# The affine part of a LayerNorm on the residual, moved from GpSimd to VectorE and cut into eighths

## The chip, the cores and the metric

The kernel runs on one core of one Trainium2 chip. The metric is the time of one execution of the whole program, in microseconds of the device. A core has five engines that run beside each other, each in its own order and held back only by semaphores: TensorE (PE in the profile) multiplies matrices, VectorE (DVE) works element by element, ScalarE (ACT) evaluates functions and copies, GpSimd (POOL) is a second elementwise engine, and SyncE (SP) issues most of the transfers.

## The reference

Two layers, each of a half-step SwiGLU FFN, a token mixer and a second FFN, on 512 tokens of width 1024. Each sub-layer ends in a LayerNorm:

```python
y = swiglu(modulate(x, mod, 0), ffn_w_in[l, 0], ffn_w_out[l, 0])
x = layer_norm(DN_ALPHA * x + 0.5 * sub_gate(mod, 0) * y, ln_g[l, 0], ln_b[l, 0])
y = token_mixer(modulate(x, mod, 1), ...)
x = layer_norm(DN_ALPHA * x + sub_gate(mod, 1) * y, ln_g[l, 1], ln_b[l, 1])
...
def layer_norm(x, g, b):
    y = (x - mu) * rsqrt(var + LN_EPS)
    return y * g + b
```

The last step, `y * g + b`, is the affine part. Its result has two readers: the modulated input of the next sub-layer, and the residual `DN_ALPHA * x` that the next sub-layer's output is added to. Inside the mixer an indexer scores keys and selects the 128 best per query, three branches (pooling, sparse attention, a gated recurrence) run on one input projection, and their projections are merged by gates.

## The kernel before

The residual lives in SBUF for the whole run, as eight tiles `xt[t][h]`: four blocks of 128 tokens, each in two halves of 512 channels. All products are done in three passes of float32r matmuls: a weight is split into `whi` (ScalarE, `split`, L371) and `wlo` (VectorE, L372), an activation likewise, and `mm3` (L387) issues high by high, high by low and low by high. Weights come in megabyte loads named `raw` or `raw_d` (L284), two buffers; the split halves have three buffers (`hp`, L204). A *unit* is one split weight and its products; the driver at the end (L1163) emits the split of the next unit before the products of the present one.

`row_units` (L416) makes a product whose output stands by token, `ps_d`, in two halves of 512 channels. It opens four PSUM banks of a pool of four (`pm`, L207), one for each token block. For the FFN each half has 11 units, for the mixer's output projection four. At the end of a half `consume` (L705) multiplies by the gate, adds it to `ALPHA * xt`, takes statistics, and after the second half normalises `xt` without the affine part. The next sub-layer's input is then made by `prep_half` (L544), which transposes the normalised `xt` and folds `ln_g` and `ln_b` into its own scales (`prep_scales`, L535). So only the residual still needs the affine part, and it needs it by the next `consume`.

`affine` (L679) does that: four broadcast loads (`lng`, `lnb`, two halves each, on SP), then for each of the eight tiles a multiply and an add, 16 instructions of 128x512 on GpSimd. It is called at the end of `entry` (L599), that is right after the first three units of a sub-layer. There are five calls: for two mixers and three FFNs. The first FFN of layer 0 has none.

What stands beside this work: at a mixer's entry VectorE begins the indexer (L894). Eight heads' scores are added up in `sel` tiles of 256, 384 and 512 columns (L918, 24 instructions of SCALAR_TENSOR_TENSOR), and then 16 rounds of `max` and `match_replace` run over them. The splits `wlo` of the input projection stand between these in VectorE's order. At an FFN's entry VectorE accumulates the conditioning for later sub-layers (`ada_acc`, L291 to 315).

In the mixer's branch stage `branch(d)` (L853), for d = 0 to 7, makes three products `ps_br`, each in a bank of the same pool of four. VectorE multiplies each with a gate (L863) and so frees its bank, GpSimd adds them up (L865, two adds a unit), and the sum is split in `mgh` (ScalarE) and `mgl` (VectorE). Units 0 and 1, and 2 and 3, are each followed by six gate units; 4 to 7 run one behind another and go straight into the output projection.

The order within an engine is made by a scheduler, from a priority order with a cost model for pacing (`Pace`, L79); an instruction marked `keep_in_program_order` keeps its place. An engine waits at the head of its queue: what stands behind a waiting instruction waits too. All engine instructions go through one helper, so the profile gives them L163; they are told apart by their tiles.

Of the kernel before, what the change touches and what calls it, by code (L numbers as in the profile page):

```python
# [14 lines left out]
ALU = mybir.AluOpType  # L15
# [7 lines left out]
KT = D // P  # L23
NTOK = T // P
NFF = DFF // P
# [149 lines left out]
def kernel(  # L175
# [23 lines left out]
    V, S, G, PE = (Paced(pace, e, n) for e, n in ((nc.vector, "V"), (nc.scalar, "S"), (nc.gpsimd, "G"), (nc.tensor, "PE")))  # L199
# [11 lines left out]
    def slot(name, dt=F32):  # L211
        return wp.tile([P, T], dt, name=name, tag="w")

    def bank(name):
        return pm.tile([P, 512], F32, name=name, tag="mm")
# [143 lines left out]
    def bcast(row, name):  # L359
        res = []  # L360
        for h in range(2):
            b = slot(name)
            nc.sync.dma_start(b, row[:, h * 512:h * 512 + 512].broadcast_to([P, 512]))
            res.append(b)
        return res
# [9 lines left out]
    def split_slot(src, name):  # L375
        hi, lo = slot(name + "h", F32R), slot(name + "l", F32R)
        S.activation(hi, src, AF.Copy)
        V.tensor_tensor(lo, src, hi.bitcast(F32), op=ALU.subtract)
        return hi, lo
# [36 lines left out]
    def row_units(pairs, nk, Wd, n, w, consume, tail=4):  # L416

        for dh in range(n):
            ps, held = [], []
            for k0 in range(0, nk, 4):  # L420
                kn = min(4, nk - k0)
                r = once(lambda k0=k0, kn=kn, dh=dh: load_raw(Wd[k0 * P:(k0 + kn) * P, dh * w:dh * w + w], kn, w, "raw_d"))
                for o in range(0, kn, 2):
                    def mm(wt, kb=k0 + o, dh=dh, ps=ps, held=held):
                        if not ps:
                            ps += [bank("ps_d") for _ in range(NTOK)]
                        held.append((kb, wt))
                        if nk - tail <= kb < nk - 2:
                            return
                        for t in range(NTOK):  # L430
                            tt = slice(t * P, t * P + P)
                            for kb_, (hi, lo) in held:
                                for i in range(2):
                                    ah, al = pairs[kb_ + i]
                                    mm3(ps[t][:, 0:w], (ah[:, tt], al[:, tt]), (row(hi, i, slice(0, w)), row(lo, i, slice(0, w))), kb_ + i == 0, kb_ + i == nk - 1)
                            if kb == nk - 2:
                                consume(dh, t, ps[t])
                        held.clear()

                    kept = n > 1 and dh == n - 1 and k0 + o >= nk - tail  # L440
                    yield (lambda r=r, o=o, kept=kept: split_rows(r()[:, o:o + 2]) if kept else split(r()[:, o:o + 2], [P, 2, w])), mm


    xt = [[None, None] for _ in range(NTOK)]
# [136 lines left out]
    def entry(l, j, xs, units, evict):  # L581

        ws, pss = [], []

        def first(wt, i):
            if i == 0:
                xs.extend(nxt[l, j][0])
                pace.join(nxt[l, j][2])
            ws.append(wt)
            pss.append(bank("ps_e"))  # L590
            m = wt[0].shape[2]
            proj_T(wt, xs, pss[i][0:m, 0:256], tok=slice(0, 256))
            if i == len(units) - 1:
                pace.join(nxt[l, j][3])
                for n, w in enumerate(ws):
                    m = w[0].shape[2]
                    proj_T(w, xs, pss[n][0:m, 256:512], tok=slice(256, 512))
                    evict(n, pss[n])
                affine(l if j else l - 1, j - 1 if j else 2)  # L599

        for i, (sp_, _) in enumerate(units):
            yield sp_, (lambda wt, i=i: first(wt, i))
# [74 lines left out]
        late_params()  # L677

    def affine(l, j):  # L679
        gr = bcast(ln_g[l, j:j + 1], "lng")  # L680
        br = bcast(ln_b[l, j:j + 1], "lnb")
        for t in range(NTOK):
            for h in range(2):
                G.tensor_tensor(xt[t][h], xt[t][h], gr[h], op=ALU.mult)
                G.tensor_tensor(xt[t][h], xt[t][h], br[h], op=ALU.add)

    def finish(t, mv, rstd, gr, br):

# [12 lines left out]
    def residual_norm(l, j):  # L701
        stats, gate, fin = {}, [], []
        final = l == DEPTH - 1 and j == 2

        def consume(dh, t, ps):  # L705
            if not gate:
                gate.extend(bcast(gate_d.pop((l, j)), "gate"))
            if t not in stats:
                stats[t] = mp.tile([P, 2, 6], F32, name="stats", tag="stats", bufs=4)
                if final and not fin:  # L710
                    fin.extend((bcast(ln_g[l, j:j + 1], "lng"), bcast(ln_b[l, j:j + 1], "lnb")))
            tmp = slot("tmp")
            V.tensor_tensor(tmp, ps, gate[dh], op=ALU.mult)
            V.scalar_tensor_tensor(xt[t][dh], xt[t][dh], ALPHA, tmp, op0=ALU.mult, op1=ALU.add)
            V.bn_stats(out=stats[t][:, dh, :], in_=xt[t][dh])
            if dh == 1:
                mv = small(2, "mv")
                V.bn_aggr(out=mv, in_=stats[t])
                rstd = small(1, "rstd")
                G.tensor_scalar(rstd, mv[:, 1:2], LN_EPS, None, op0=ALU.add)  # L720
                G.tensor_tensor(rstd, rstd, mhalf[:, 0:1], op=ALU.pow)
                if final:
                    finish(t, mv, rstd, *fin)
                    return
                for h in range(2):
                    V.tensor_scalar(xt[t][h], xt[t][h], mv[:, 0:1], rstd, op0=ALU.subtract, op1=ALU.mult)
                if t % 2:
                    begin_next(l, j, t // 2)

        return consume  # L730


    def ffn(l, f, background):
        j = 2 * f
        xs, hT, gate_ps = [], [], {}
        W1, W2 = ffn_w_in[l, f], ffn_w_out[l, f]

        def evict(n, ps):
            if n == 0:
                background()  # L740
            if n % 2 == 0:
                gate_ps[n // 2] = ps
                return
            s = slot("s")
            S.activation(s, gate_ps.pop(n // 2), AF.Silu)
            V.tensor_tensor(s, s, ps, op=ALU.mult)
            hT.append(split_slot(s, "h"))

        def run(n):
            def mm(wt):  # L750
                ps = bank("ps_f")
                proj_T(wt, xs, ps)
                evict(n, ps)
            return mm

        units = []
        raws = (None, None) if l + j else [rp.tile([P, KT, 256], F32, name="raw", tag="raw") for _ in range(2)]
        for i in (range(0, NFF, 2) if l + j else range(3, NFF, 2)):
            m = min(2, NFF - i)
            g, u = (list(col_units(W1, o + i * P, m * P, [run(2 * (i + a) + b) for a in range(m)])) for b, o in enumerate((0, DFF)))  # L760
            units += [v for pair in zip(g, u) for v in pair]
        if l + j:
            yield from entry(l, j, xs, units[0:3], evict)
        else:
            entry0(xs, W1, raws, evict)
        yield from units[3 if l + j else 0:]
        yield from row_units(hT, NFF, W2, 2, 512, residual_norm(l, j), 6)


    def mixer(l):  # L770
# [77 lines left out]
            S.activation(g, ps, AF.Tanh, scale=0.5)  # L848
            gates[d, b] = g

        merged, ys = [], []

        def branch(d):  # L853
            def mm(wt):
                if not ys:
                    pace.join(*tasks.values())
                    ys.extend(ya + yb + [y for _, y in sorted(yc, key=lambda y: y[0])])
                m = None
                for b, (k0, nk) in enumerate(((0, 2), (2, 2), (4, 4))):
                    ps = bank("ps_br")  # L860
                    proj_T(wt, ys, ps, k0=k0, nk=nk)
                    g = gates.pop((d, b))
                    V.scalar_tensor_tensor(g, g, 1.0, ps, op0=ALU.add, op1=ALU.mult)  # L863
                    if m is not None:
                        G.tensor_tensor(g, g, m, op=ALU.add)  # L865
                    m = g
                merged.append(split_slot(m, "mg"))
            return mm

        def gate_units(i):  # L870
# [17 lines left out]
        for i in range(4):  # L888
            yield from col_units(w_branch[l], i * 256, 256, [branch(2 * i), branch(2 * i + 1)])
            if i + 2 < 4:  # L890
                yield from gate_units(i + 2)
        yield from row_units(merged, KT, w_out[l], 2, 512, residual_norm(l, 1), 6)

    def indexer(st, wi, kh, kl, qiT):  # L894

# [267 lines left out]
    for sp_, mm in trunk():  # L1163
        wt = sp_() if sp_ else None
# [31 lines left out]
```

## Time and profile before

| What | Value |
|---|---|
| median of 3 runs | 2462.33 us (2460.08 to 2465.26) |
| the profiled execution | 2459.55 us, span 2457.8 us |
| busy: PE, DVE, ACT, POOL | 2376.6, 1455.0, 809.5, 366.0 us |
| of POOL, the instructions `x<-x,lng` and `x<-x,lnb` | 140.6 us, 86 instructions, 80 of them in `affine` |

The span runs from the first to the last instruction. A busy engine of 97% need not be one without waits: what matters is where its idle time lies and what ended it.

### The profile page before, as it was taken

Reading aid. Unit: us, or ns where it says so; the run is one execution under the profiler, and the core shown is the slowest. Engines: PE = TensorE matmul, PEld = TensorE weight load, DVE = VectorE, ACT = ScalarE, POOL = GpSimd, SP = SyncE. Lnnn points to the kernel's source line nnn. Section 1 sums busy time; section 2 is a strip of 40 time slices with the busy share of each in tenths; the row PEclk is TensorE's granted clock in tenths of the full one; section 3 lists DMA queues with packets and bytes.
Section 4 is the critical chain, followed back from the end, with each engine's and each line's share of the span. In section 5 each row is a group of like instructions: output and inputs, shape, how many; then the busy total and the mean of one; then the engine's idle time right before and its main releaser. Section 6 shows DMA issues by size and latency. Waiting matters only on the chain.

```text
span 2457.8 us, 28856 instructions
## 1 busy us (share of the span) xinstructions
PE 2376.6 (97%) x11333; PEld 1980.4 (81%) x11333; DVE 1455.0 (59%) x2197; ACT 809.5 (33%) x1209; POOL 366.0 (15%) x354
## 2 busy tenths in 40 slices
PE   6999999899999999999999999998999999999997
PEld 5788888687888887888887888886878888888886
DVE  6666766978533678532478664479684347533334
ACT  3322223354432232322232322242644322332221
POOL 0000000316300231000031000030452011400002
PEclk9999999999999999999999999999999999999999
DMA  7575642222223346323346554322222232333331
GB/s 244 188 244 185 236 163 83 69 86 87 70 71 101 112 145 212 123 87 111 119 149 212 187 191 143 124 69 70 75 84 65 86 103 95 103 103 103 115 105 63
DMA packets 241768, 306.11 MB, mean 125 GB/s; under 512 B 12380, under 2 KB 172860, under 8 KB 241632
## 3 DMA queue, kind: packets, MB, share of 16 engines
q1 hardware_dynamic: 241440, 304.24, 37.6%
q8 instruction: 89, 1.46, 0.3%
q14 instruction: 47, 0.39, 0.0%
q0 software_dynamic: 192, 0.03, 0.0%
HBM read 302.10 MB, written 3.44 MB: 124 GB/s over the span
## 4 chain that ended last, share of the span: by engine, by line
PE 74%; DVE 11%; issue 6%; DMA 3%; ACT 3%; POOL 2%; SPq 1%; POOLq 0%; DVEq 0%; ACTq 0%
PE ps_f L163 32%; PE ps_d L163 21%; PE ps_m L163 11%; PE ps_e L163 4%; PE ps_br L163 4%; DVE sel L163 2%; DVE wlo L163 2%; DMA ada_raw<-in_w_ada_dram 1%; DVE ada_acc L163 1%; DMA raw<-in_ffn_w_in_dram 1%; DVE m L163 1%; PE ps_x L163 1%; ACT L163 1%; DVE x L163 1%; DMA ada<-in_w_ada_dram 1%
## 5 line engine op out<-in xcount | busy, mean ns | idle before, releaser
L163 DVE TENSOR_TENSOR wlo<-raw,whi 128x1024 fp32r<-128x1024 f32 (+2 forms) x292 | 365.3, 1253 | 382.3 <-ACT whi L163 375.4
L163 ACT ACTIVATE whi<-raw 128x1024 fp32r<-128x1024 f32 (+2 forms) x292 | 299.0, 1029 | 713.1 <-PE ps_f L163 396.3
L163 PE MATMUL ps_f<-xh,wlo 128*128 128x512 f32 x1288 | 503.1, 391 | 4.3 <-DVE wlo L163 4.3
L163 PE MATMUL ps_f<-xh,whi 128*128 128x512 f32 x1288 | 503.9, 391 | 2.9 <-ACT s L163 2.9
L163 PE MATMUL ps_f<-xl,whi 128*128 128x512 f32 x1288 | 502.6, 390 | 0.0
L163 PEld LDWEIGHTS ps_f<-xh,wlo 128*128 128x128 f32 x1288 | 242.3, 188 | 57.2 <-DVE wlo L163 6.9
L163 PEld LDWEIGHTS ps_f<-xh,whi 128*128 128x128 f32 x1288 | 242.3, 188 | 54.8 <-ACT s L163 3.3
L163 PE MATMUL ps_m<-xh,whi 128*128 128x512 f32 x704 | 284.3, 404 | 0.0
L163 PEld LDWEIGHTS ps_f<-xl,whi 128*128 128x128 f32 x1288 | 242.4, 188 | 49.4
L163 PE MATMUL ps_m<-xl,whi 128*128 128x512 f32 x704 | 276.8, 393 | 0.0
L163 PE MATMUL ps_m<-xh,wlo 128*128 128x512 f32 x704 | 275.5, 391 | 0.0
L163 PE MATMUL ps_d<-whi,hh 128*128 128x512 f32 x608 | 236.9, 390 | 0.0
L163 PE MATMUL ps_d<-whi,hl 128*128 128x512 f32 x608 | 236.8, 390 | 0.0
L163 PE MATMUL ps_d<-wlo,hh 128*128 128x512 f32 x608 | 236.8, 389 | 0.0
L163 DVE TENSOR_TENSOR wlo<-raw_d,whi 128x1024 fp32r<-128x1024 f32 (+1 forms) x102 | 126.9, 1244 | 182.4 <-ACT whi L163 181.8
L163 ACT ACTIVATE whi<-raw_d 128x1024 fp32r<-128x1024 f32 (+1 forms) x102 | 104.7, 1026 | 342.5 <-PE ps_d L163 283.9
L163 DVE SCALAR_TENSOR_TENSOR ada_acc<-ada_raw,condT,ada_acc 128x512 f32<-128x512 f32 x224 | 181.7, 811 | 13.5 <-DMA ada_raw<-in_w_ada_dram 7.6
L163 PEld LDWEIGHTS ps_m<-xh,wlo 128*128 128x128 f32 x704 | 132.3, 188 | 28.4 <-DVE wlo L163 0.5
L163 PEld LDWEIGHTS ps_m<-xh,whi 128*128 128x128 f32 x704 | 132.8, 189 | 24.2 <-issue 0.5
L163 PEld LDWEIGHTS ps_m<-xl,whi 128*128 128x128 f32 x704 | 132.7, 188 | 23.7 <-issue 1.0
L163 DVE TENSOR_TENSOR s<-s,ps_f 128x512 f32<-128x512 f32 x82 | 55.7, 679 | 147.2 <-PE ps_f L163 147.1
L163 PEld LDWEIGHTS ps_d<-whi,hh 128*128 128x128 f32 x608 | 114.2, 188 | 23.8
(254 smaller groups left out, 3452.6 us busy)
## 6 DMA issues: line engine op xcount, KB each, us to landing
raw<-in_ffn_w_in_dram SPq DMA_DIRECT2D x84, 1024.0 KB, 5.1
ada_raw<-in_w_ada_dram SPq DMA_DIRECT2D x256, 256.0 KB, 5.9
raw<-in_mix_w_in_dram SPq DMA_DIRECT2D x46, 1024.0 KB, 5.4
raw_d<-in_ffn_w_out_dram SPq DMA_DIRECT2D x40, 1024.0 KB, 5.1
ada<-in_w_ada_dram SPq DMA_DIRECT2D x32, 256.0 KB, 5.2
raw<-in_w_branch_dram SPq DMA_DIRECT2D x8, 1024.0 KB, 5.0
raw_d<-in_w_out_dram SPq DMA_DIRECT2D x8, 1024.0 KB, 5.0
raw_d<-in_ffn_w_out_dram SPq DMA_DIRECT2D x8, 512.0 KB, 3.7
```

The source lines that it names most:

```text
L163: ins = f(*a, **k)
```

## The change

`affine` becomes a generator. It is no longer called in `entry`. Its first step issues the four broadcasts, and each of its next eight steps does one tile (one eighth) with a multiply and an add on VectorE, marked to keep their place. It works on the same normalisation as before (the argument shift moved inside). In an FFN one step is taken behind each unit of the down projection (`beside`), so all eight are done by the ninth of 22 units. In the mixer the first step and seven eighths are taken behind the eight branch units, the last eighth behind the first unit of the output projection.

```diff
-                affine(l if j else l - 1, j - 1 if j else 2)
...
     def affine(l, j):
+
+        l, j = (l, j - 1) if j else (l - 1, 2)
+        if l < 0:
+            return
         gr = bcast(ln_g[l, j:j + 1], "lng")
         br = bcast(ln_b[l, j:j + 1], "lnb")
-        for t in range(NTOK):
-            for h in range(2):
-                G.tensor_tensor(xt[t][h], xt[t][h], gr[h], op=ALU.mult)
-                G.tensor_tensor(xt[t][h], xt[t][h], br[h], op=ALU.add)
+        yield
+        for h in range(2):
+            for t in range(NTOK):
+                for r, op in ((gr, ALU.mult), (br, ALU.add)):
+                    tc.keep_in_program_order(V.tensor_tensor(xt[t][h], xt[t][h], r[h], op=op))
+                yield
+
+    def beside(units, gen):
+
+        def go(mm):
+            def f(wt):
+                mm(wt)
+                next(gen, None)
+            return f
+
+        for sp_, mm in units:
+            yield sp_, go(mm)
...
-        yield from row_units(hT, NFF, W2, 2, 512, residual_norm(l, j), 6)
+        yield from beside(row_units(hT, NFF, W2, 2, 512, residual_norm(l, j), 6), affine(l, j))
...
-        merged, ys = [], []
+        merged, ys, aff = [], [], affine(l, 1)
...
                 merged.append(split_slot(m, "mg"))
+                next(aff)
...
-        yield from row_units(merged, KT, w_out[l], 2, 512, residual_norm(l, 1), 6)
+        yield from beside(row_units(merged, KT, w_out[l], 2, 512, residual_norm(l, 1), 6), aff)
```

On GpSimd, at the first mixer's entry, the 16 instructions of `affine` stood between the `rstd` of the normalisation and the first work of the recurrence (`hproj`, `Eq`):

```order
 L163 TENSOR_SCALAR rstd<-mv 128x1
 L163 TENSOR_TENSOR rstd<-rstd,mhalf 128x1
-L163 TENSOR_TENSOR x<-x,lng 128x512 x4
-L163 TENSOR_TENSOR x<-x,lnb 128x512 x4
-L163 TENSOR_TENSOR x<-x,lng 128x512 x2
-L163 TENSOR_TENSOR x<-x,lnb 128x512 x2
-L163 TENSOR_TENSOR x<-x,lng 128x512 x2
-L163 TENSOR_TENSOR x<-x,lnb 128x512 x2
 L163 TENSOR_SCALAR hproj<-hproj,omlb 128x512
 L163 TENSOR_TENSOR Eq<-lf 128x512
```

They are gone there, and nothing takes their place on GpSimd.

On VectorE, at the end of the first mixer's branch stage, this stands from unit 6's `mgl` on (`gate<-gate,ps_br` frees a bank; the second `mgl` is unit 7's):

```order
 L163 TENSOR_TENSOR mgl<-gate,mgh 128x512
-L163 SCALAR_TENSOR_TENSOR gate<-gate,ps_br 128x512 x3
+L163 TENSOR_TENSOR x<-x,lng 128x512
+L163 SCALAR_TENSOR_TENSOR gate<-gate,ps_br 128x512
+L163 TENSOR_TENSOR x<-x,lnb 128x512
+L163 SCALAR_TENSOR_TENSOR gate<-gate,ps_br 128x512
+L163 TENSOR_TENSOR x<-x,lng 128x512
+L163 SCALAR_TENSOR_TENSOR gate<-gate,ps_br 128x512
+L163 TENSOR_TENSOR x<-x,lnb 128x512
 L163 TENSOR_TENSOR wlo<-raw_d,whi 128x1024
 L163 TENSOR_TENSOR mgl<-gate,mgh 128x512
+L163 TENSOR_TENSOR x<-x,lng 128x512
```

Two eighths stand between the three multiplies of unit 7, and a third one begins behind its `mgl`; its add and the last `wlo<-raw_d` of the half follow. Behind the `mgl` of units 4 and 5 stands one eighth each, its multiply ahead of the next unit's first gate multiply and its add ahead of the second.

On SP the broadcasts move with the steps. In the second FFN of layer 0 they stand behind the third load of the down projection's weights, ahead of the gate's broadcast:

```order
 L286 DMA raw<-in_ffn_w_in_dram 128x8x256 x10
 L286 DMA raw_d<-in_ffn_w_out_dram 128x4x512 x3
+L363 DMA lng<-in_ln_g_dram 128x512 x2
+L363 DMA lnb<-in_ln_b_dram 128x512 x2
 L363 DMA gate<-gd_2_2982 128x512 x2
```

At the FFN's entry, where they stood among loads of `ada_raw`, they are gone. The order of TensorE's instructions is the same as before throughout.

## Rows read from the trace of the kernel before

**Rows 1.** The page, part 1: busy us (share of the span) xinstructions.

```profile
PE 2376.6 (97%) x11333; PEld 1980.4 (81%) x11333; DVE 1455.0 (59%) x2197; ACT 809.5 (33%) x1209; POOL 366.0 (15%) x354
```

**Rows 2.** Windows: stretch, length, busy PE, PEld, DVE, ACT, POOL, clock, DMA.

```profile
460.00:560.00 100.00, 88.70 (x401) 73.56 (x399) 83.16 (x185) 47.81 (x58) 14.30 (x13) 0.95 0.25 76
```

**Rows 3.** PE's waits at the two mixers' and two FFNs' entries: total, times, longest.

```profile
PE ps_d L163 <- DVE wlo L163: 11.2, 1, 11.2
...
PE ps_d L163 <- DVE wlo L163: 10.1, 1, 10.1
...
PE ps_f L163 <- DVE wlo L163: 2.3, 3, 1.1
...
PE ps_f L163 <- DVE wlo L163: 2.0, 3, 0.8
```

**Rows 4.** Timeline of PE, first mixer: start, duration, instruction, idle before.

```profile
471.55 0.80 PE L163 MATMUL ps_d<-wlo,xh 128*128 128x512 f32 x1 [11.21 <-DVE wlo L163]
```

**Rows 5.** Timeline of DVE at the first mixer's entry.

```profile
435.80 1.91 DVE L163 TENSOR_TENSOR wlo<-raw_d,whi 128x1024 fp32r<-128x1024 f32 x1 [1.78 <-ACT whi L163]
...
440.50 5.63 DVE L163 SCALAR_TENSOR_TENSOR sel<-relu,wiN,sel 128x256 f32<-128x256 f32 x4
...
447.62 9.07 DVE L163 SCALAR_TENSOR_TENSOR sel<-relu,wiN,sel 128x256 f32<-128x256 f32 x6
...
462.05 0.42 DVE L163 MAX8 m<-sel 128x8 f32<-128x256 f32 x1
...
470.29 1.21 DVE L163 TENSOR_TENSOR wlo<-raw_d,whi 128x1024 fp32r<-128x1024 f32 x1
```

**Rows 6.** Timeline of POOL at the first mixer's entry.

```profile
432.83 6.02 POOL L163 TENSOR_TENSOR x<-x,lng 128x512 f32<-128x512 f32 x4 [22.48 <-issue]
...
453.24 3.04 POOL L163 TENSOR_TENSOR x<-x,lnb 128x512 f32<-128x512 f32 x2
```

**Rows 7.** DVE by form: 439.5 to 455.9 us, then 1665.3 to 1672 us (POOL idle).

```profile
L163 DVE SCALAR_TENSOR_TENSOR sel<-relu,wiN,sel 128x256 f32<-128x256 f32 x7 | 9.9, 1408 | 0.4
...
L163 DVE SCALAR_TENSOR_TENSOR sel<-relu,wiN,sel 128x512 f32<-128x512 f32 x5 | 3.7, 736 | 0.0
L163 DVE SCALAR_TENSOR_TENSOR sel<-relu,wiN,sel 128x384 f32<-128x384 f32 x5 | 3.0, 606 | 0.0
```

**Rows 8.** Timeline of ACT at the first mixer's entry.

```profile
440.75 8.15 ACT L163 ACTIVATE relu<-ps_sc 128x256 f32<-128x256 f32 x19 [0.18 <-PE ps_sc L163]
```

**Rows 9.** Windows of 2 us behind the first mixer's wait.

```profile
472.00:474.00 2.00, 2.00 (x6) 1.52 (x6) 2.00 (x3) 0.00 (x0) 0.00 (x0) 0.50 0.67 130
474.00:476.00 2.00, 2.00 (x8) 1.59 (x7) 2.00 (x8) 0.67 (x2) 0.00 (x0) 0.65 1.07 377
```

**Rows 10.** DVE by form at an FFN's entry, 904 to 934 us.

```profile
L163 DVE TENSOR_TENSOR wlo<-raw,whi 128x1024 fp32r<-128x1024 f32 x4 | 7.5, 1871 | 0.0
```

**Rows 11.** The chain, first mixer: branch units 4 to 7, then the output projection.

```profile
804.02 21.76 PE ps_br L163 x96
825.78 21.84 PE ps_d L163 x96
```

**Rows 12.** Timelines of DVE and POOL in the same stretch.

```profile
819.49 1.88 DVE L163 SCALAR_TENSOR_TENSOR gate<-gate,ps_br 128x512 f32<-128x512 f32 x3
...
825.06 0.69 DVE L163 TENSOR_TENSOR mgl<-gate,mgh 128x512 fp32r<-128x512 f32 x1 [1.85 <-ACT mgh L163]
...
832.55 1.23 DVE L163 TENSOR_TENSOR wlo<-raw_d,whi 128x1024 fp32r<-128x1024 f32 x1 [0.25 <-ACT whi L163]
...
820.85 3.52 POOL L163 TENSOR_TENSOR gate<-gate 128x512 f32<-128x512 f32 x2 [2.67 <-DVE gate L163]
```

**Rows 13.** Tile `lng`, on DVE (at the run's end): duration in ns, min, median, max.

```profile
L163 DVE TENSOR_TENSOR x<-x,lng x1: 692/692/692, 2453.4 to 2453.4; 128x512 f32<-128x512 f32 x1
```

**Rows 14.** Down projection, second FFN of layer 0: timelines of SP and DVE.

```profile
1120.90 0.97 SPq L363 DMA_DIRECT2D gate<-gd  x2
...
1130.33 1.23 DVE L163 TENSOR_TENSOR wlo<-raw_d,whi 128x1024 fp32r<-128x1024 f32 x1 [3.85 <-ACT whi L163]
```

## The prediction

> **What bounds the kernel now.** I read the page first: PE is busy for 2376.6 of 2457.8 us [rows 1], so at most 81 us are to be had without taking work from PE, and the order of PE's instructions stays. What the change can win or lose is waits of PE. The windows by stage come next: in 460 to 560 us, behind the first mixer's entry, PE is busy for 88.70 of 100 us, and the granted clock is 0.95 [rows 2]. PE's waits there are a single one: 11.2 us, for a `wlo` of VectorE. The second mixer has its twin, 10.1 us, and the entries of two FFNs have 2.3 and 2.0 us in three short ones each [rows 3]. These are 25.6 us, and all of them stand where `affine` runs on GpSimd or just behind it.
>
> The timelines say why. PE resumes at 471.55, so it stopped at about 460.3 [rows 4]. The `wlo` that it waited for ran from 470.29 to 471.50; VectorE took it late because it was still at the indexer, without a gap [rows 5]. GpSimd's affine instructions ran from 432.83 to 456.28 [rows 6]. In that time a `sel` instruction of 256 columns took 1408 ns, and without GpSimd one of 384 columns takes 606 and one of 512 takes 736 [rows 7]. The smaller instruction takes twice as long as the larger, so VectorE is held up by GpSimd. At an FFN's entry the same is seen: `wlo` has a mean of 1871 ns beside `affine` [rows 10], and 1.23 us elsewhere [rows 14].
>
> The Trainium skill, "SBUF — State Buffer", section "Who interferes with whom", gives this as a rule: a VectorE instruction with two SBUF inputs and a GpSimd instruction that reads SBUF exclude each other for a whole instruction. The rows above agree. The rule also speaks against the change, since all 80 moved instructions have two SBUF inputs and will meet GpSimd's gate adds; that is weighed under the rivals.
>
> **Part 1: GpSimd's 80 instructions go from the entries.** In the first mixer 20 `sel` instructions lie between 440.50 and the first MAX8 at 462.05: 21.55 us [rows 5], namely 7 of 256, 8 of 384 and 5 of 512 columns. Alone, 512 takes 0.736 and 384 takes 0.606; carried on, 256 takes 0.476 [rows 7]. The sum is 3.3 + 4.8 + 3.7 = 11.9 us, and 10.2 if each overlaps the next by 0.08 (three instructions that follow one another take 1.88 in all [rows 12]). So the MAX8 comes 9.7 to 11.3 us earlier. The `wlo` at 435.80 takes 1.91 [rows 5] and would take 1.23, 0.7 less. Together VectorE is 10.4 to 12.0 us ahead; I take 12.0, since back-to-back instructions do overlap. Is something else late then? ScalarE has its last `relu` at 448.90 [rows 8], and VectorE alone would be at its MAX8 at about 451, so it isn't held up by ScalarE. From MAX8 to the awaited `wlo` 8.2 us stay, and it would end at 459.5 to 461.1, against PE's need at 460.3. The wait goes, or leaves at most 0.8.
>
> PE also ran slowly behind the wait: the granted clock is 0.50 in 472 to 474 and 0.65 in the next 2 us [rows 9], which cost 1.0 + 0.7, and 0.2 before 472: 1.9 us. With the wait that is 13.1, but what follows in the mixer waits for VectorE too, and that gains 12.0 only. I take 12. The second mixer is alike with a wait 1.1 shorter: 11. Bounds for both: 19 (VectorE's 9.7 and as much less in the second) to 25 (wait and clock whole).
>
> In the two FFNs' entries 2.3 + 2.0 = 4.3 us go, since `wlo` falls back to 1.23 and the four broadcasts leave the queue of `ada_raw`. Bounds: 2 (waits for transfers stay) to 4.3; I take 4.3.
>
> **Part 2: 80 instructions more on VectorE.** Alone one takes 0.692 us [rows 13], so 55 us are added to VectorE's 1455; what counts is where.
>
> *Down projections, three FFNs, 8 pairs each.* A unit has 24 matmuls as a branch unit has, 5.44 us on PE [rows 11]; VectorE has a `wlo` of 1.23 in it and sat idle for 3.85 ahead of it [rows 14]. A pair is 1.38. It is covered, and a `wlo` that came late by a pair would still be ahead, since the split halves have three buffers. The broadcasts are issued where the gate's stood, at 1120.90 [rows 14], and the first pair stands behind a unit's products, some 5 us later; should they land later than that, the idle 3.85 takes it up. Cost 0; without that cover it would be a pair for each unit, 1.4 x 24 = 33 us, for which no row speaks. The gate's broadcast comes some 2 us later and is read only at the half's end.
>
> *Branch stage, two mixers.* Units 0 to 3 have six gate units of 5.44 us behind each two, so a pair there costs nothing. Units 4 to 7 are another matter. They last 21.76 / 4 = 5.44 us each on PE [rows 11]. VectorE's loop is already longer: from the three gate multiplies at 819.49, over GpSimd's two adds (820.85 to 824.37), to the end of `mgl` at 825.75 [rows 12], about 6.2 us, for `mgl` stands ahead of the next unit's multiplies. With a pair behind each `mgl` (1.25 with overlap) the first multiply of the next unit is 0.6 later and the other two, and so the adds and the next `mgl`, 1.25. This adds up: unit 5 has 0.6 and 1.25, unit 6 has 1.85 and 2.5, unit 7's first multiply 3.1. Four banks go round, so a product needs the multiply of the fourth product before it. Two things become late:
> - The second bank of the output projection is due at 825.78 + 1.36 = 827.1 [rows 11]. It is freed by unit 7's first multiply, which ended at about 819.49 + 6.2 + 0.6 = 826.3 [rows 12] and now ends at 829.4. With 0.3 us that PE has lost by then (unit 7's second bank, due at 821.7, free at 822.0), PE waits for 2.0. Unit 0 of the projection then ends at 833.5 in place of 831.2.
> - The last `wlo` of the half ended at 833.78 [rows 12] and was needed at 825.78 + 5.44 + 2.72 + 0.23 = 834.2: 0.4 to spare. Now unit 7's `mgl` is 3.7 to 4.3 later, an eighth stands behind it, and the `wlo` ends at about 838. PE needs it at 833.5 + 2.95 = 836.4: a wait of 1.6.
>
> So 0.3 + 2.0 + 1.6 = 3.9 a mixer, 7.8 in all. Bounds: 0 (the banks turn in another order and the multiplies keep their slack) to 14 (each pair costs what it would beside GpSimd, 1.41 in place of 0.48 [rows 7], some 0.9 an instruction).
>
> **Sum.** 12 + 11 + 4.3 - 7.8 = 19.5 us less. The profiled execution took 2459.55, so 2440; the median of the runs lies 2.8 above it, so 2442.8. I predict 2442.
>
> **The rivals.**
> 1. *The branch run costs nothing.* For it: VectorE still sits idle for 1.85 us ahead of an `mgl` [rows 12], and a bank may be free sooner than the round-robin says. Against it: the loop of 6.2 us in 5.44. Time: 2462.3 - 27.3 = 2435.
> 2. *VectorE stays late at the mixers.* Half of the gain of part 1 is eaten, since the 8.2 us of MAX8 and match work ahead of the `wlo` stay and the `sel` chain may then be fed by PE and ScalarE rather than run at its own rate. Against it: the last `relu` at 448.90. Time: 2462.3 - 11.5 - 4.3 + 7.8 = 2454.
> 3. *Slower: the port is lost in the branch run.* Every moved instruction between units 4 and 7 meets one of GpSimd's adds and waits one out (3.52 / 2 = 1.76 us [rows 12]); two in each unit make the loop 6.2 + 1.25 + 3.5 = 11 in place of 5.44. Four units give 22, less the slack of 5.4: 16.8 a mixer, 33.6 in all, and 2462.3 - 27.3 + 33.6 = 2468.6. It decides from 13.7 us a mixer on. For it: the adds and the pairs are in the same 5.44 us. Against it: by the order both instructions of the pairs behind units 4 and 5 come ahead of the multiply that starts the second add, so GpSimd is idle then; only the pair inside unit 7 meets it.
>    The rule of the Trainium skill named above says the same with who comes first: by it that one pair in unit 7 costs an add's rest for each instruction, some 1 to 2 us a mixer, and the sum would be 2445.
> 4. *The slow `sel` has another cause than GpSimd.* Then nothing is won and the branch run costs 7.8: 2470. Rows 7 speak against it.
>
> **How the numbers follow.** Forecast 0.62 (its own range 2434 to 2450), rival 1 0.18, rival 2 0.13, rival 3 0.04, rival 4 0.03. What a measurement of this kernel can tell from no change is about 0.2%, 5 us: faster below 2457.4, slower above 2467.2. The forecast and rivals 1 and 2 lie below the first bound, less 0.02 for the upper tail of rival 2: faster 0.91. Rivals 3 and 4 make slower, some of them falling within the bound: slower 0.05, same 0.04. For 8 in 10 the range takes in the forecast's, rival 1 and the middle of rival 2: 2431 to 2454. By the bounds alone it would be 2462.3 - 29.3 = 2433 to 2462.3 - 21 + 14 = 2455.
>
> **What would show it.** Right: in the first mixer no wait of PE for a `wlo` over 1 us behind the scores, `sel` instructions of 256 columns at about 0.48 us, and a clock that stays at 1.00 there; no waits of `ps_f` for `wlo` at the FFNs' entries; new waits of PE of some 2 us for `gate` and 1.6 for `wlo` around the end of the branch stage; none in the down projections. Wrong: a wait of several us left at the mixers' entry (the chain was fed by ScalarE or PE), or waits in the down projections for `x` or the broadcasts, which I cost at nothing.

## The result and the profile after

The changed kernel takes 2434.10 us (median of 4 runs, 2432.84 to 2435.23) against 2461.24 us for the kernel before in the same comparison (4 runs, 2460.08 to 2465.26). The ratio is 0.9889, with a 95% interval of 0.9877 to 0.9900: 27.1 us less by the medians, where 19.5 less were forecast. The time lies at the low end of the forecast's own range (2434 to 2450). The profiled execution took 2433.21 us, its span 2431.4 against 2457.8, so 26.4 less. All times below are in us.

Part 1 of the page (busy, share of the span, instructions):

```profile
PE 2369.7 (97%) x11333; PEld 1974.5 (81%) x11333; DVE 1453.8 (60%) x2277; ACT 809.6 (33%) x1209; POOL 234.4 (10%) x274
```

VectorE has 80 instructions more than in [rows 1], of some 0.69 each, 55 in all, and its busy time is 1.2 lower. So about 56 of its busy time before were no work of its own but instructions stretched beside GpSimd's; experiment 3, which has neither, is busy on VectorE for 1399.7, that is 55.3 less than before.

**Where PE lost time and where no longer.** PE's waits at the first mixer's entry (440 to 470), at the second's (1635 to 1660) and at the end of the first branch stage (785 to 835), as total, times, longest:

```profile
PE ps_d L163 <- DVE wlo L163: 0.5, 1, 0.5
...
PE ps_d L163 <- DVE wlo L163: 0.6, 1, 0.6
...
PE ps_d L163 <- DVE gate L163: 1.7, 1, 1.7
PE ps_d L163 <- DVE wlo L163: 1.4, 1, 1.4
PE ps_br L163 <- DVE gate L163: 0.2, 1, 0.2
```

The first two lines answer to the 11.2 and 10.1 of [rows 3]. The last three are new; the second branch stage has 1.6, 1.4 and 0.3. At the two FFNs' entries PE has no wait at all. The first of these windows (stretch, length, busy PE, PEld, DVE, ACT, POOL, clock, DMA), at the first of the two FFNs, shows PE busy without a gap and GpSimd silent, and the second, behind the first mixer's entry, a granted clock of 1.00 (the level of 2.4 GHz) from the awaited matmul at 457.81 on, where [rows 9] had 0.50 (1.2 GHz) after PE had stood still for 11.2:

```profile
882.00:937.00 55.00, 55.00 (x254) 45.90 (x253) 42.79 (x56) 18.68 (x24) 0.00 (x0) 1.00 0.68 236
...
457.00:459.00 2.00, 1.49 (x7) 1.02 (x6) 2.00 (x4) 0.00 (x0) 0.00 (x0) 1.00 0.11 10
```

**The first mixer's entry.** VectorE's timeline (start, duration, instruction) answers to [rows 5]:

```profile
433.48 1.23 DVE L163 TENSOR_TENSOR wlo<-raw_d,whi 128x1024 fp32r<-128x1024 f32 x1 [1.77 <-ACT whi L163]
...
437.40 2.25 DVE L163 SCALAR_TENSOR_TENSOR sel<-relu,wiN,sel 128x256 f32<-128x256 f32 x4
...
448.31 0.41 DVE L163 MAX8 m<-sel 128x8 f32<-128x256 f32 x1
...
456.56 1.20 DVE L163 TENSOR_TENSOR wlo<-raw_d,whi 128x1024 fp32r<-128x1024 f32 x1
```

From the first `sel` to the first MAX8 there are 10.91 in place of 21.55; the `wlo` ahead of them is back at 1.23. By form, in 436 to 450, the instruction that had 1408 ns beside GpSimd's `affine` [rows 7] now has 481 (count, then busy, mean ns):

```profile
L163 DVE SCALAR_TENSOR_TENSOR sel<-relu,wiN,sel 128x512 f32<-128x512 f32 x6 | 4.4, 740 | 0.0
L163 DVE SCALAR_TENSOR_TENSOR sel<-relu,wiN,sel 128x384 f32<-128x384 f32 x7 | 4.3, 608 | 0.0
L163 DVE SCALAR_TENSOR_TENSOR sel<-relu,wiN,sel 128x256 f32<-128x256 f32 x7 | 3.4, 481 | 0.4
```

**The end of the branch stage.** In [rows 11] the chain that ended last went straight through PE there. Now it goes round VectorE, GpSimd and ScalarE (start, duration, what):

```profile
788.54 5.23 PE ps_br L163 x23
...
804.51 0.69 DVE mgl L163
805.20 0.60 DVE x L163
805.80 0.60 DVE gate L163
806.40 0.60 DVE x L163
807.00 0.61 DVE gate L163
807.61 0.07 issue
807.68 1.31 POOL gate L163
808.99 0.07 issue
809.05 2.16 POOL gate L163
811.22 0.02 issue
811.24 0.64 ACT mgh L163
811.88 0.02 issue
811.90 0.69 DVE mgl L163
...
822.65 12.54 PE ps_d L163 x54
```

From one `mgl` to the next the loop takes 811.90 - 804.51 = 7.39, and two `x` of 0.60 are in it: without them it would be 6.19, the 6.2 that stood in the prediction. PE makes a unit in 5.44, so each of these units puts VectorE further behind, until a bank is freed late. VectorE's timeline has the rest:

```profile
811.90 0.69 DVE L163 TENSOR_TENSOR mgl<-gate,mgh 128x512 fp32r<-128x512 f32 x1 [1.85 <-ACT mgh L163]
...
816.11 1.19 DVE L163 TENSOR_TENSOR x<-x,lnb 128x512 f32<-128x512 f32 x1
817.22 2.31 DVE L163 TENSOR_TENSOR wlo<-raw_d,whi 128x1024 fp32r<-128x1024 f32 x1
819.46 0.68 DVE L163 TENSOR_TENSOR mgl<-gate,mgh 128x512 fp32r<-128x512 f32 x1
```

VectorE still sits idle for 1.85 ahead of the `mgl`, and the pair stands just behind it, where it delays what comes next. Of the moved instructions in this run one, at 816.11, lies beside an add of GpSimd's; it takes 1.19 in place of 0.69. The `wlo` behind it takes 2.31, but its twin in the kernel before, beside the same adds, took as much:

```profile
827.46 2.29 DVE L163 TENSOR_TENSOR wlo<-raw_d,whi 128x1024 fp32r<-128x1024 f32 x1
```

**The account.** Both kernels issue the same 11333 matmuls in the same order, so the start of each was compared with that of its twin, and PE's lead read off stage by stage. The changed kernel is 2.3 ahead by 131 us, long before the programs differ; at the same matmul experiment 2 is 0.2 behind the kernel before and experiment 4 is 2.1 behind, so that is one execution's spread. From there on:

| Stretch | PE's lead grows by | forecast |
|---|---|---|
| first mixer, a short wait of the scores (`ps_sc`) for VectorE, listed with 0.4 before | 0.7 | 0 |
| first mixer's entry: wait and clock | 12.5 | 12 |
| first branch stage's end | -4.2 | -3.9 |
| the normalisation behind it | 1.2 | 0 |
| the entries of two FFNs | 3.2 + 2.9 | 4.3 |
| second mixer, the short wait of the scores | 0.9 | 0 |
| second mixer's entry: wait and clock | 11.0 | 11 |
| second branch stage's end | -4.3 | -3.9 |
| sum | 23.9 | 19.5 |

With the 2.3 that is 26.2 (26.3 at the last matmul, unrounded), and 26.4 by the spans.

### The profile page after: what moved, and what is told of

Read it like the earlier page. It is cut to its first block, busy times and chain, and to the rows that moved or that the text cites. A ratio compares the mean times of both kernels' runs of the same rounds, so it can differ in the third digit from the quotient of the medians.

```text
span 2431.4 us, 28810 instructions
## 1 busy us (share of the span) xinstructions
PE 2369.7 (97%) x11333; PEld 1974.5 (81%) x11333; DVE 1453.8 (60%) x2277; ACT 809.6 (33%) x1209; POOL 234.4 (10%) x274
## 4 chain that ended last, share of the span: by engine, by line
PE 80%; DVE 11%; ACT 3%; POOL 3%; issue 2%; DMA 1%; SPq 0%; POOLq 0%; ACTq 0%; DVEq 0%
PE ps_f L163 36%; PE ps_d L163 21%; PE ps_m L163 13%; PE ps_e L163 4%; PE ps_br L163 2%; DVE sel L163 2%; DVE wlo L163 2%; DVE x L163 1%; DVE m L163 1%; ACT L163 1%; PE ps_x L163 1%; DMA ada<-in_w_ada_dram 1%; PE ps_ao L163 1%; POOL rstd L163 1%; POOL gate L163 1%
## 5 line engine op out<-in xcount | busy, mean ns | idle before, releaser
L163 DVE TENSOR_TENSOR wlo<-raw,whi 128x1024 fp32r<-128x1024 f32 (+2 forms) x292 | 356.4, 1223 | 384.5 <-ACT whi L163 372.5
L163 DVE SCALAR_TENSOR_TENSOR ada_acc<-ada_raw,condT,ada_acc 128x512 f32<-128x512 f32 x224 | 168.2, 751 | 12.1 <-DMA ada_raw<-in_w_ada_dram 6.2
L163 PEld LDWEIGHTS ps_m<-xl,whi 128*128 128x128 f32 x704 | 132.6, 188 | 23.9 <-issue 1.0
L163 PEld LDWEIGHTS ps_d<-whi,hh 128*128 128x128 f32 x608 | 114.1, 188 | 23.9
```

The costliest lines, as they stand in the source:

```text
L163: ins = f(*a, **k)
```

## The experiments

Diffs are against the changed kernel unless another is named. The first four ran in one comparison, beside one set of runs of the kernel before (median 2464.42, 7 runs, 2459.27 to 2467.07); the last two in another (2459.98, 15 runs, 2458.00 to 2463.37).

**1. The new places, the old engine.** The eighths stay where the change put them, but on GpSimd.

```diff
-                    tc.keep_in_program_order(V.tensor_tensor(xt[t][h], xt[t][h], r[h], op=op))
+                    tc.keep_in_program_order(G.tensor_tensor(xt[t][h], xt[t][h], r[h], op=op))
```

> The changed kernel with one word different: the eighths stay on GpSimd, at the new places. My theory (the place is what counts: beside the score sums and the splits at an entry GpSimd's reads hold VectorE up, behind the units of the down projection nobody waits): the entries keep their 31 us (13 + 12 + 3 + 3). In units 4 to 7 of the branch stage GpSimd then has its two adds (3.5 us) and a pair (2.6 to 3.3 us) in a loop of 6.2 us, so the loop stays at 6.2 to 6.8 and costs 0 to 3 us a mixer: 2428 to 2434. Rival (it is the engine, the 0.69 us of a VectorE instruction in place of 1.66): the slow GpSimd instructions would hold up the splits in the down projections as they did at the entries, and the time is 2450 to 2461.

Measured: 2435.02 (2433.01 to 2435.67), ratio 0.9885 (0.9868 to 0.9901), the same as the change. So the gain comes from the place, and the move to VectorE is no part of it that can be measured. GpSimd does stretch VectorE's splits in the down projection; this `wlo`, beside an add of GpSimd's that began at 1116.29, takes 2.36 where the changed kernel has 1.23:

```profile
1116.31 2.36 DVE L163 TENSOR_TENSOR wlo<-raw_d,whi 128x1024 fp32r<-128x1024 f32 x1 [3.85 <-ACT whi L163]
```

But VectorE sat idle for 3.85 ahead of it, and PE has no wait in these products. In the branch stage the GpSimd version loses less (its waits at the end of the first one):

```profile
PE ps_d L163 <- DVE wlo L163: 0.9, 1, 0.9
PE ps_d L163 <- DVE gate L163: 0.8, 1, 0.8
```

There the eighth stands in GpSimd's queue, behind its two adds, and the loop takes 6.6, from one `mgl` to the next (807.64, 814.24, 820.85), and PE loses 2.6 a mixer by matched matmuls. The other half of the separation, VectorE at the old place, wasn't tried.

**2. The same eighths behind the gate units.** In the mixer the steps are taken behind the twelve gate units, where VectorE waits for PE, and none in the run of units 4 to 7.

```diff
-                next(aff)
...
-                yield from gate_units(i + 2)
-        yield from beside(row_units(merged, KT, w_out[l], 2, 512, residual_norm(l, 1), 6), aff)
+                yield from beside(gate_units(i + 2), aff)
+        yield from row_units(merged, KT, w_out[l], 2, 512, residual_norm(l, 1), 6)
```

> The changed kernel, but in the mixer the steps stand behind the twelve gate units that follow branch units 1 and 3, not behind the branch units, so that none lies in units 4 to 7. My theory (a pair in the loop of VectorE, GpSimd and ScalarE there makes the loop 7.4 us long and costs PE 4.0 and 4.1 us): both costs go, 2434.1 - 8.1 = 2426. Rival (the two waits at the output projection would come from elsewhere, since the loop is 6.2 us without the pairs): under 2 us are won, 2432 to 2434.

Measured: 2427.45 (2426.66 to 2429.82), ratio 0.9857 (0.9843 to 0.9872). This version beats both kernels: its interval lies below that of the change. At the end of the branch stage PE has no wait, the loop is back at 6.19 (`mgl` at 805.93 and 812.12), and the chain goes through PE alone, as in [rows 11]:

```profile
791.07 21.76 PE ps_br L163 x96
812.83 21.77 PE ps_d L163 x96
```

By matched matmuls PE loses less than 0.1 in either branch stage. The ratios differ by 0.0032, which is 7.9 of 2462, against 8.5 in the account and 7.8 in the forecast; each ratio is uncertain by 3 to 4 us, so the size rests on the matched matmuls.

**3. No affine part at all.** The broadcasts and the arithmetic are left out, so the residual lacks `ln_g` and `ln_b`.

```diff
-        gr = bcast(ln_g[l, j:j + 1], "lng")
-        br = bcast(ln_b[l, j:j + 1], "lnb")
...
-                for r, op in ((gr, ALU.mult), (br, ALU.add)):
-                    tc.keep_in_program_order(V.tensor_tensor(xt[t][h], xt[t][h], r[h], op=op))
```

> The changed kernel with the affine part left out wholly, loads and arithmetic (so the residual lacks ln_g and ln_b). It is the floor: what the part costs where it now stands. My theory (covered everywhere but in branch units 4 to 7): 2426, the same as with the steps behind the gate units. Rival (the pairs and the broadcasts also cost in the down projections or through VectorE's later start of other work): 2420 or less.

Measured: 2428.83 (2427.11 to 2429.42), ratio 0.9860 (0.9846 to 0.9875). That is the floor, and experiment 2 stands on it: 80 instructions on VectorE and 20 loads cost nothing that can be measured when they stand where VectorE is idle.

**4. GpSimd busy, but only writing.** The kernel before, with the 16 instructions replaced by 48 fills of the tiles `lng` and `lnb`, which read nothing; the affine part is left out.

```diff
-                G.tensor_tensor(xt[t][h], xt[t][h], gr[h], op=ALU.mult)
-                G.tensor_tensor(xt[t][h], xt[t][h], br[h], op=ALU.add)
+                for s in (gr[h], br[h]):
+                    for _ in range(3):
+                        G.memset(s, 0.0)
```

> The kernel before, with affine's 16 GpSimd instructions replaced by 48 fills of its four broadcast tiles (so the affine part is left out): GpSimd is busy for about as long (0.53 us each, 25 us) at the same place but reads nothing from SBUF. My theory (what holds VectorE up is that GpSimd reads SBUF while VectorE reads two operands from it): the score sums of 256 columns fall from 1.41 to 0.48 us, the waits of 11.2 and 10.1 us go, and the time is 2461.2 - 31 = 2430, up to 2434 as the broadcasts stay in the queue at the FFNs' entries. Rival (any work of GpSimd holds VectorE up, or the loads do): 2455 to 2462.

Measured: 2429.68 (2428.00 to 2432.01), ratio 0.9865 (0.9851 to 0.9880), the floor again. GpSimd is busy in 433.84 to 456.8, about as long as in [rows 6]. VectorE by form in 440 to 455, beside the fills:

```profile
L163 DVE SCALAR_TENSOR_TENSOR sel<-relu,wiN,sel 128x256 f32<-128x256 f32 x7 | 3.4, 483 | 0.4
L163 DVE TENSOR_SCALAR sel<-kc 128x128 f32<-128x128 f32 x1 | 0.6, 646 | 0.0
```

So it was not GpSimd's being busy that held up the `sel` chain, but its reading. The same holds at the FFNs' entries, where this version keeps the broadcasts at their old place: by matched matmuls PE gains 3.2 and 2.1 there, of the change's 3.2 and 2.9. So the waits there came from the reads, and the broadcasts in the queue of `ada_raw`, which the forecast named beside them, had at most the 0.8 that is missing. The Trainium skill, "SBUF — State Buffer", section "Who interferes with whom", says the same: a GpSimd instruction that only writes SBUF doesn't shut out a VectorE instruction with two SBUF inputs. The rows agree, with 483 ns beside fills and 1408 beside multiplies. The last row is an instruction with one input that the fills do hold up: 646 ns, against 0.22 us in the changed kernel at 435.55, with GpSimd idle. The same section has that for `tensor_scalar` in a mode that uses both of VectorE's ports; the trace agrees that it is held up, and that it ran in this mode is not shown. At the second FFN's entry another such instruction, which takes 0.48 elsewhere, waited through nearly the whole run of fills:

```profile
1270.13 9.45 DVE L163 TENSOR_SCALAR ada_acc<-ada_raw,condT 128x512 f32<-128x512 f32 x1
```

From 1259.5 on the fills followed one another without a gap. The instruction ended at 1279.58, just behind the first gap of 0.06 between two of them (1279.29 to 1279.35). One wait of PE's, 0.5, was left at this entry; that it comes from here is not shown.

**5. The pair inside the idle time.** The step is taken ahead of the split, so that the pair stands behind the three gate multiplies, in VectorE's idle 1.85, but beside GpSimd's adds.

```diff
+                next(aff)
                 merged.append(split_slot(m, "mg"))
-                next(aff)
```

> The changed kernel with each mixer step taken ahead of the split of the unit's sum, so that on VectorE the pair stands behind the unit's three gate multiplies and around a wlo, where VectorE waited 1.85 us for mgh, and not between mgl and the next multiplies. There it runs beside GpSimd's two adds. My theory (GpSimd's reads and VectorE's two-operand instructions exclude each other): the pair doesn't fit into the 1.85 us, since its instructions and wlo wait the adds out; mgl comes 1 us or more late and the loop is 7.0 to 7.4 us as in the changed kernel, with x instructions of 1.2 us and more, 2431 to 2436. Rival (the loop is only a matter of order, and idle time ahead of mgl takes the pair of 1.25 us for nothing): the loop stays at 6.2, x instructions at 0.69, the waits at the output projection go, 2427.

Measured: 2432.50 (2430.60 to 2433.70), ratio 0.9891 (0.9876 to 0.9906). The time lies in the first theory's range (2431 to 2436), and the rival's 2427 would be a ratio of 0.9861, below the interval. The trace says why, and bears out neither wholly. The loop is 6.55 (`mgl` at 801.04, 807.60 and 814.15), between the 6.2 of the rival and the 7.0 to 7.4 of the first theory, and PE loses 2.4 a mixer at the branch's end, in place of 4.2. VectorE and GpSimd in one turn of it:

```profile
808.20 1.87 DVE L163 SCALAR_TENSOR_TENSOR gate<-gate,ps_br 128x512 f32<-128x512 f32 x3
809.99 1.40 DVE L163 TENSOR_TENSOR x<-x,lng 128x512 f32<-128x512 f32 x1
811.32 2.31 DVE L163 TENSOR_TENSOR wlo<-raw_d,whi 128x1024 fp32r<-128x1024 f32 x1
813.55 0.68 DVE L163 TENSOR_TENSOR x<-x,lnb 128x512 f32<-128x512 f32 x1
814.15 0.68 DVE L163 TENSOR_TENSOR mgl<-gate,mgh 128x512 fp32r<-128x512 f32 x1
...
809.55 2.99 POOL L163 TENSOR_TENSOR gate<-gate 128x512 f32<-128x512 f32 x2 [3.56 <-DVE gate L163]
```

The multiply beside the first add takes 1.40 in place of 0.69, the `wlo` beside the second 2.31, where it takes 1.23 alone and 1.94 in the changed kernel's turn (at 808.12), and VectorE has no idle time left. So the meeting with the adds that rival 3 spoke of is real, but its price is 0.7 for an instruction, not 1.76, and most of it is paid in time that was idle: with the pair the loop is 0.36 longer than the 6.19 without it.

**6. The FFNs alone.** The mixers keep `affine` on GpSimd at their entries; the three FFNs are as in the change.

```diff
+                if j == 1:
+                    affine_old(l, 0)
...
-                next(aff)
...
-        yield from beside(row_units(merged, KT, w_out[l], 2, 512, residual_norm(l, 1), 6), aff)
+        yield from row_units(merged, KT, w_out[l], 2, 512, residual_norm(l, 1), 6)
```

(`affine_old` is the removed function.)

> Only the three FFNs get the change; in the two mixers affine stays on GpSimd at the entry. My theory (a listed wait of PE is counted from the modelled end of the matmul before, 0.39 us after its start, though the next could start after 0.23; three waits an entry thus cost 3.2 and 2.9 us, not the 2.3 and 2.0 listed): PE is ahead by 6.1 us behind both FFN entries and by no more anywhere else, 2461 - 6 = 2455, with waits of 11.2 and 10.1 us still in the mixers. Rival (the listed waits are the cost, and the rest of what was seen there is the run's own spread): 4.3 ahead, 2457. A third way (taking affine from the FFNs alone already brings mixers ahead): under 2450.

Measured: 2454.77 (11 runs, 2451.89 to 2457.08), ratio 0.9978 (0.9970 to 0.9987), so 5.4 less (3.2 to 7.4), which alone can't tell 6.1 from the rival's 4.3. By matched matmuls PE gains 3.2 and 2.9 at the two FFNs' entries, 6.1 in all, as with the whole change. At the mixers the long waits are back. The kernel's largest sum of waits, then that of the first and the second mixer's entry:

```profile
PE ps_d L163 <- DVE wlo L163: 22.2, 4, 10.2
...
PE ps_d L163 <- DVE wlo L163: 10.2, 1, 10.2
...
PE ps_d L163 <- DVE wlo L163: 10.1, 1, 10.1
```

## Why the prediction was right, point by point

**Mixers' entries, forecast 12 + 11, measured 12.5 + 11.0.** The mechanism is shown: `sel` is fast without GpSimd's reads (481 ns, and 483 beside its writes), the MAX8 comes 13.7 earlier, of which 3.1 had been gained by the first `sel` (437.40 against 440.50), so 10.6 (forecast 9.7 to 11.3), and 0.5 is left of the wait (forecast at most 0.8). At the first entry PE's lead grows by 10.7 at the awaited matmul and by 1.8 while the kernel before runs at a low clock behind it (forecast 1.9). A short wait of the scores in each mixer, which goes too, was not in the sum: 0.7 + 0.9.

**FFNs' entries, forecast 4.3, measured 6.1, and 6.1 in experiment 6 too.** This is the mis-sized term. The waits listed were taken as PE's loss. The list counts a wait from the modelled end of the matmul before, 0.39 after its start, while without a wait the next one starts 0.227 after it (24 in 5.44). So each listed wait is 0.16 short. The matmul behind a wait also holds up the next one, which starts 0.34 after it in place of 0.23. In the kernel before:

```profile
930.95 0.51 PE L163 MATMUL ps_f<-xh,wlo 128*128 128x512 f32 x1 [1.06 <-DVE wlo L163]
931.29 0.40 PE L163 MATMUL ps_f<-xh,whi 128*128 128x512 f32 x1
```

That is 0.11 more for each wait, seen behind all six. Six times 0.27 are 1.6 of the missing 1.8. The same two terms sit in the branch's waits: 3.3 are listed, 4.2 were lost, and three times 0.27 are 0.8 of the difference. Of the two reasons that the forecast gave for this term, experiment 4 bears out the first, the `wlo` back at 1.23.

**Down projections, forecast 0, measured 0.** PE has no wait in them. The first pair did wait for its broadcast, as the working allowed, and the next `wlo` still had idle time to spare:

```profile
1112.10 0.69 DVE L163 TENSOR_TENSOR x<-x,lnb 128x512 f32<-128x512 f32 x1 [0.72 <-DMA lnb<-in_ln_b_dram]
1114.63 1.23 DVE L163 TENSOR_TENSOR wlo<-raw_d,whi 128x1024 fp32r<-128x1024 f32 x1 [1.83 <-ACT whi L163]
```

**Branch stage, forecast 3.9 a mixer (0.3 + 2.0 + 1.6), measured 4.2 and 4.3 (listed 0.2 + 1.7 + 1.4).** Places, owners and sizes of the three waits came as worked out, since the loop was followed round with its new length (7.45 expected, 7.39 measured). Experiment 2 takes them away and nothing else.

**The rivals.** Rival 1 named 2435, near the measured time, but for another reason: the branch waits it denied are there, and the time is as low in the main because part 1 was worth more (by 3.9), and for the rest by spread and by the 1.2 below, whose cause is open. Rival 2 falls with the 0.5 that is left of the waits. Rival 3 falls in its size: one moved instruction a mixer met an add, as the order had told, and paid 0.5 (1.19 in the first, 1.19 in the second, for 0.69); the rule of the Trainium skill beside it would have added 1 to 2 a mixer, and what is seen is this 0.5, with nothing more on the `wlo` behind it in the first mixer (2.29 before, 2.31 after) and 0.3 in the second (2.00 before, 2.31 after), inside a wait that the forecast had at 1.6 and that is listed with 1.4. The 0.5 follows from the order in time: the instruction met an add that had 0.64 left. Rival 4 falls with experiments 3 and 4.

**What the sum missed.** Between the forecast's 19.5 and the 26.4 of the two profiled executions lie 6.9: 2.3 are the spread of their beginnings, 1.6 the short waits of the scores, 0.5 the mixers' entries, 1.8 the FFNs' entries and 1.2 the normalisation behind the first mixer; 0.7 goes the other way, in the branch stages. That makes 6.7; the last 0.2 is rounding and what lies outside the matmuls. The 1.2 is the clock's: it dips behind a normalisation in which PE waits for 2.8 to 2.9 in both kernels, and the dip lies otherwise in the two executions. Windows of 4 us, of the kernel before and then of the change:

```profile
868.00:872.00 4.00, 3.34 (x16) 3.34 (x17) 2.98 (x7) 1.79 (x5) 0.02 (x1) 0.50 0.35 132
```

```profile
857.00:861.00 4.00, 3.56 (x18) 3.37 (x19) 3.44 (x8) 2.36 (x7) 0.00 (x0) 0.65 0.32 117
```

PE's lead grows there by 2.9 in experiment 6, which has the old mixers, by 1.6 in experiment 2, by 1.7 in experiment 3 and by nothing in experiment 4. So the size doesn't follow the edit, and whether the change has a part in it is open.

## What to carry to other kernels

Ask of helper work first where it stands, and only then which engine does it: the affine part cost some 34 us (ratio 0.986 without it) beside VectorE work that PE was waiting for, and nothing that can be measured where VectorE was idle, while at the new places the engine made no difference to the time (VectorE at the old places wasn't tried). A stage that is a closed loop over several engines has idle time to give only where an engine in it waits: the pair behind `mgl` made the loop 1.2 longer (7.39), the pair in the idle 1.85 ahead of it 0.36 (6.55). Add the new work to the loop's length and compare that with the bottleneck's step, or put it where the engine waits for the bottleneck, as experiment 2 did for another 7 to 8 us. A list of waits undercounts: take the start of one instruction to the start of the next.

## What the runs showed of the hardware that was not expected

- A VectorE instruction with two SBUF inputs that meets one of GpSimd's loses what is left of that one, less 0.14. In experiment 5 the multiply at 809.99 had 0.85 of an add ahead of it (to 810.84) and lost 0.71; in the changed kernel the `x` at 816.11 had 0.64 and lost 0.50; in experiment 1 the `wlo` at 1116.31 had 1.27 and lost 1.13. So the price of a meeting hangs on when it begins, and the whole add of rival 3 (1.76) is too much. Beside `affine` a `sel` of 256 columns lost 0.93, and GpSimd's adds took 1.5 each (two in 3.04 [rows 6]) in place of the 1.30 that one took in experiment 1.
- GpSimd loses by the same measure. Its two adds took 3.52 with a `wlo` beside them [rows 12], and 2.99 with a multiply and a `wlo` beside them in experiment 5. The second add began with 1.00 left of the `wlo` in the one (822.21 to 823.21) and with 0.47 left of the multiply in the other (810.92 to 811.39); it took 2.15 and 1.62, where an add alone takes 1.29.
- A one-input instruction of VectorE's of 0.48 took 9.45 beside back-to-back fills (experiment 4), so fills are harmless to the instructions with two inputs seen here and not to every neighbour.
- A wait of PE's costs more than is listed for it: 0.16 by the way it is counted, and 0.11 in the start of the second matmul behind it.
